# A second run of Strassen quads in a decoder trunk's output projections

## The chip, the cores and the metric

The kernel runs on one core of one Trainium2 chip. The metric is the device time of one execution in microseconds, from the median of several runs; less is better. Engines are named as in the profile: PE (TensorE), PEld (its weight loads), DVE (VectorE), ACT (ScalarE), POOL (GpSimd) and SP (the queue that issues most loads). Each engine takes its own list of instructions in order.

## The reference

Two decoder layers over 256 tokens of width 2048, all in float32. Each layer is attention, an output projection `attn @ w_o`, a residual with layer norm, a gated feed-forward with a width-3 convolution, its down projection, and another residual with layer norm:

```python
for layer in range(DEPTH):                                  # DEPTH = 2
    attn = moba_attention(h, ..., moba_w_o) or swa_attention(..., swa_w_o)
    ...                                                     # both end in  o.reshape(B, S, ATT_WIDTH) @ w_o
    h = layer_norm(ALPHA * h + attn, ln_g[layer, 0], ln_b[layer, 0])
    ffn = conv_ffn(h, w_up, conv_w, conv_b, w_down)
    h = layer_norm(ALPHA * h + ffn, ln_g[layer, 1], ln_b[layer, 1])
```

The change is in the two output projections: 256 x 2048 times 2048 x 2048, one after each attention.

## The kernel before, in words

**Three products for one.** Each float32 factor is held as a high part (`wh`, rounded to the fast format) and a low part (`wl`, what is left). A product is three matmuls that add into one PSUM bank: high by high, high by low, low by high (L502 to L504). The weights stream from HBM in *halves* of 128 x 1024 (two blocks of 128 x 512, 512 KB). SP loads a half into one of six `raw` buffers, ACT copies it to `wh` (L173), DVE subtracts to get `wl` (L182). This pair is called the *split* of a half. `wh` and `wl` have four buffers, so as a rule the split of half i + 4 waits until PE is done with half i. Before the end of a projection the list `reach` lets the splits run further ahead: halves then go into parts of `xT`, `st` and `up` that stand empty.

**Tokens and chunks.** The 256 tokens are two tiles (t = 0, 1) of 128, and the 2048 output columns are four chunks (n = 0 to 3) of 512. A *plain* half is multiplied with both token tiles: 2 blocks x 2 tiles x 3 = 12 matmuls.

**Quads.** Where two contraction blocks, two chunks and the two token tiles meet, the kernel may use a Strassen scheme with 7 products in place of 8. Two quads are worked off as seven *mixed* halves (`SEVEN`), each with 2 x 3 = 6 matmuls. Three of the seven come from the weights themselves and four (T1 to T4) from sums of weight blocks. `presums` makes these sums in earlier stages on DVE (L449, four of 128 x 512 for a quad), and sends them through HBM (`gb` in, `ws` out on POOL, `ws` back in as `raw`). The token side needs sums too: `sums` makes them per pair of quads from the attention's output (`st`) and puts them in `xT` (`whole` L539, `combine` L550, `split` L555 and L556).

**Folding.** In a run of quads, PSUM holds P1, P5, P6 and P7 for the chunk pair (tiles named `at`, four banks) beside the direct results (tiles `acc`, four banks). When the pair's quads are done, `fold` adds the four into the residual `res` in three steps (`first`, `second`, `third`), each run behind one more half. `into` does one such addition, and a BN_STATS (L623) when the last part of a token tile and chunk has come. A bank is free for the next user when its last reader is done. `evac` adds a direct result to `res`.

**Order.** All orders are written out by hand: `at(n, f)` puts `f` n halves later, and `take` first issues the splits up to the half now wanted plus three (or `reach`), then what `at` has due. What was put in first is in the engine's list first.

An output projection has 38 halves before (numbered from 0 here): 5 plain, 7 mixed, 3 plain and 7 mixed for chunks 0 and 1 (four quads), then 16 plain halves for chunks 2 and 3. The last eight are the *window*: all eight with t = 0 first, and then all with t = 1, so that tile 0's norm (`late`: `evac`, `moments`, `norm`, L630 to L642) and the transposes for the next stage (`turn`, L675) can start while PE does t = 1. In the window the splits run ahead to the first six halves of the next stage.

Attention's last steps hang over into the first halves of the projection; the last head's `values` (L824, L825) and `outputs` (ACT L829, DVE L830) are of these, and they hold one of the four `at` banks.

Of the kernel before, what the change touches and what calls it, by code (L numbers as in the profile page):

```python
# [47 lines left out]
NQ = 12  # L48
PLAINS = ((5, 2, 2, 2, 2, 0, 6), (0, 1, 1, 1, 1, 0, 15))
NQ_O = 4  # L50
PLAINS_O = (5, 3, 0)
IN_PARTS = (True, True)
NV = 2 * 8 + 4 * 8
SEVEN = (("B11", "B21"), ("T1", "T3"), ("T2", "T4"), ("B22", "B22"), ("B11", "B21"), ("T1", "T3"), ("T2", "T4"))
# [19 lines left out]
    return plan  # L74


PLAN_O = _mixed(0, PLAINS_O, _plain(range(NH - 2 * NQ_O), (0, 1)), NH // 2 - NQ_O) + _plain(range(NH), (2, 3))
PLAN_V = _mixed(1, PLAINS_O, _plain(range(KB - 2 * NQ_O), (2, 3)), KB // 2 - NQ_O)
PLAN_DOWN = [h for c in range(2) for h in _mixed(c, PLAINS[c], _plain(range(2 * NQ, FT), (2 * c, 2 * c + 1)), 0)]
QUADS = {}  # L80
for _l in range(2):
    QUADS[2 * _l] = [(2 * _l, 0, NH // 2 - NQ_O + p) for p in range(NQ_O)]
    QUADS[2 * _l + 1] = [(2 * _l + 1, c, p) for c in range(2) for p in range(NQ)]
QUADS[4] = [(4, 1, KB // 2 - NQ_O + p) for p in range(NQ_O)]
ORDER = [q for li in (4, 0, 1, 2, 3) for q in QUADS[li]]
AHEAD_OF = {0: QUADS[4] + QUADS[0] + QUADS[1][:2], 1: QUADS[1][2:] + QUADS[2], 2: [], 3: QUADS[3]}


def _summed(half):
# [22 lines left out]
def trunk(ctx: ExitStack, tc: tile.TileContext, wst, wsum, xT_in, x_in, relb, onehot, umask, sinks, conv_in, ln_g, ln_b, out):  # L112
# [353 lines left out]
    def mixed(src, plan, p0, ns, quad_blocks, place, into):  # L466

        banks, used, owed = {}, {}, {}

        def token(x, t):  # L470
            return x[:, t * P:(t + 1) * P], x[:, T + t * P:T + (t + 1) * P]

        def keys(e):
            b, k, n = e
            if b == "plain":
                return [(n, t) for t in range(2)]
            n0, n1 = 2 * n, 2 * n + 1
            return [{"B11": ("P1", n), "B21": (n0, 0), "T1": ("P5", n), "T3": ("P7", n), "T2": ("P6", n), "T4": (n0, 1),
                     "B22": (n1, 0)}[b]]

        def target(e):
            b, k, n = e
            if b == "plain":
                return [(key, *token(src(k), t)) for t, key in enumerate(keys(e))]
            k1, k2, far = src(2 * k), src(2 * k + 1), place((k - p0) // 2)
            far = [tuple(far[:, h, k % 2, j, :] for h in range(2)) for j in range(ns)]
            s1, s3, s4, s2 = (far[0], token(k1, 1), *far[1:]) if ns == 3 else far
            return [(*keys(e), *{"B11": token(k1, 0), "B21": token(k2, 0), "T1": s1, "T3": s3, "T2": s2,
                                 "T4": token(k2, 1), "B22": s4}[b])]

        for half in plan:
            for e in half:
                for key in keys(e):
                    owed[key] = owed.get(key, 0) + 1

        def product(key, sh, sl, wh, wl):
            if key not in banks:
                banks[key] = psum.tile([P, 512], F32, name="at" if key[0] in SUMS else "acc")
                used[key] = 0
            acc, first, last = banks[key], used[key] == 0, used[key] == owed[key] - 1  # L500
            used[key] += 1
            nc.tensor.matmul(acc, sh, wh, start=first, stop=False)  # L502
            nc.tensor.matmul(acc, sh, wl, start=False, stop=False)  # L503
            nc.tensor.matmul(acc, sl, wh, start=False, stop=last)  # L504

        def done(*keys):
            return all(used.get(key) == owed[key] for key in keys)

        def fold(c):
            n0, n1 = 2 * c, 2 * c + 1  # L510
            p1, p5, p6, p7 = (banks.pop((b, c)) for b in SUMS)
            w = tmpp.tile([P, HW], F32, name="tmp")
            u, v = w[:, 0:512], w[:, 512:HW]

            def first():
                nc.scalar.activation(u, p1, AF.Copy)
                into(0, n0, u)
                nc.vector.tensor_tensor(out=u, in0=p6, in1=u, op=ALU.add)
                nc.vector.tensor_tensor(out=v, in0=p5, in1=u, op=ALU.add)

            def second():
                into(0, n1, v)
                nc.vector.tensor_tensor(out=u, in0=p7, in1=u, op=ALU.add)

            def third():
                into(1, n0, u)
                into(1, n1, u)
                into(1, n1, p5)

            for i, f in enumerate((first, second, third)):  # L530
                at(1 + i, f)

        def sums(i):
            x = quad_blocks(i)
            g = []

            def whole():
                g.append(tmpp.tile([P, HW], F32, name="tmp"))
                nc.vector.tensor_tensor(out=g[0].rearrange("p (a b) -> p a b", a=4), in0=x[:, :, 0:T].bitcast(F32),  # L539
                                        in1=x[:, :, T:2 * T].bitcast(F32), op=ALU.add)  # L540

            def combine():
                a11, a21, a12, a22 = (g[0].rearrange("p (q s c) -> p s q c", q=2, s=4)[:, j] for j in range(4))
                if ns == 3:
                    ops = (a22, a22, a21, ALU.subtract), (a21, a22, a11, ALU.add), (a12, a12, a22, ALU.subtract)
                else:
                    ops = ((a21, a11, a21, ALU.subtract), (a22, a22, a21, ALU.subtract), (a11, a22, a11, ALU.add),
                           (a12, a12, a22, ALU.subtract))
                for o, a, b, op in ops:
                    nc.vector.tensor_tensor(out=o, in0=a, in1=b, op=op)  # L550

            def split():
                s = g[0].rearrange("p (q s c) -> p q s c", q=2, s=4)[:, :, 4 - ns:4, :]
                hi, lo = (place(i)[:, h] for h in range(2))
                nc.scalar.activation(hi, s, AF.Copy)  # L555
                nc.vector.tensor_tensor(out=lo, in0=s, in1=hi.bitcast(F32), op=ALU.subtract)  # L556

            return whole, combine, split

        return SimpleNamespace(banks=banks, target=target, product=product, done=done, fold=fold, sums=sums)  # L560

    def project_out(src, plan, li, homes, preload, turnover=None, quad_blocks=None):
# [13 lines left out]
        def settle():  # L576


            ring, places, following = homes()
            aside.update({w0 - len(ring) + j: x for j, x in enumerate(ring) if x})  # L580
            aside.update({w0 + j: x for j, x in enumerate(places)})
            aside.update({n0 + 4 + j: x for j, x in enumerate(following)})
            first = w0 - len(ring) - AHEAD
            for i in range(first, w0 + 3):
                reach[i] = i + min(AHEAD + (i - first) * 3 // 5, len(ring) - 1)
            for i, s in enumerate((4, 6, 7, 9, 11, 12, 13), w0 - 4):
                reach[i] = min(max(reach[i], w0 + s), n0 + 5)

        stats = stat.tile([P, 2, NCH, 6], F32, name="stats", bufs=1, padded_shape=[P, 2, NCH, 10])
        gb = gbp.tile([P, 2, D], F32, name="gb")  # L590
# [107 lines left out]

        def late(t, i):
            last = i == WINDOW - 1  # L700
            if t == 0 and last:
                evac(NCH - 1, 0)
                sd = moments(0)
                nc.vector.reciprocal(rs[0], sd)
                for c in COLS[0]:
                    norm(0, c)
            if t == 1 and after:
                if 3 <= i < 7:
                    c = COLS[0][i - 3]
                    low(0, c, turn(0, c))  # L710
                if 5 <= i < 7:
                    high_upto(n0 + i + 1)
            if t == 1 and last:
                evac(NCH - 1, 1)
                if after:
                    sd = moments(1)
                    nc.vector.reciprocal(rs[1], sd)
                else:
                    last_norm()
            if t == 1 and not after and 2 <= i < NCH + 1:  # L720
                scaled_ahead(i - 2)

        if quads:
            groups = PLAINS[0] if ns == 3 else PLAINS_O
            for i in range(len(groups) - 1):
                m = 4 if i and not groups[i] else sum(groups[:i]) + 7 * i - (ns == 3) if i else ns == 3
                for j, f in enumerate(sums(i)):
                    at(m + j, f)
        evacuated, folded = set(), set()
# [112 lines left out]
    def layer_attention(l, rest, stage, turnover):  # L842
# [65 lines left out]
        def v_pair():  # L908
# [17 lines left out]

            parted = mixed(src, PLAN_V, k0 // 2, 4, lambda i: xT[:, k0 + 4 * i:k0 + 4 * i + 4, :], place, into)
            mv = Moving(src, 0)
            for i in range(len(PLAINS_O) - 1):
                for j, f in enumerate(parted.sums(i)):  # L930
                    at(sum(PLAINS_O[:i]) + 7 * i + j, f)
            evacuated = set()
            for half in PLAN_V:
                blocks = [mv.block() for _ in range(2)]
# [53 lines left out]
    class FeedForward:  # L988
# [31 lines left out]
        def run(self, rest):  # L1020
# [62 lines left out]

            ws_opening(accs, between, opened)
            ahead = AHEAD_OF[2 * l + 1]
            presums(ahead, [4 + 152 * i // (len(ahead) - 1) for i in range(len(ahead))])
            for u in range(OPENING, 2 * FT):
                acc = acc_tile()
                ws_unit(acc)
# [137 lines left out]
```

## Time and profile before

| | before |
|---|---|
| median of three runs | 2043.67 us (2043.19 to 2043.96) |
| the profiled execution | 2042.94 us, of which its span is 2041.2 us |
| PE, PEld busy | 2034.1 us, 1759.5 us |
| DVE, ACT, POOL busy | 1722.3 us, 1162.5 us, 79.7 us |
| matmuls | 10962 |
| DMA | 578.20 MB, mean 283 GB/s |
| granted TensorE clock | 1.000 |

The profile is one execution by the hardware profiler; its own time is 0.73 us under the median of the runs. Busy times are per engine and overlap. Matmuls are pipelined: a 128 x 512 matmul has a duration of 0.39 us in the rows, but the next one starts 0.23 us later, so distances between starts are what counts. In the timeline, "x2" is two instructions in one row, and brackets show the idle time before the first and what ended it. The first output projection lies at 292 to 381 us, the second at 1240 to 1331 us.

### The profile page before, as it was taken

The numbers are of one execution on the slowest core, as the hardware profiler recorded it, in microseconds if no ns is written. First come the engines' busy times: TensorE is split into PE (matmuls) and PEld (weight loads), VectorE is DVE, ScalarE is ACT, GpSimd is POOL, SyncE is SP. The second block draws the span as 40 slices with busy tenths as digits, with TensorE's granted clock in tenths as the row PEclk, the third lists the DMA queues.
The fourth block names the chain that finished last, engine by engine and source line by source line (L and its number), as shares of the span: only waits on it lengthen the run. The fifth ranks groups of instructions, "written<-read, shape, count | busy, mean of one in ns | idle before, by whom it ended". The sixth has DMA issues, their size and how long they took to land.

```text
span 2041.2 us, 30207 instructions
## 1 busy us (share of the span) xinstructions
PE 2034.1 (100%) x10962; PEld 1759.5 (86%) x10962; DVE 1722.3 (84%) x2520; ACT 1162.5 (57%) x1762; POOL 79.7 (4%) x146
## 2 busy tenths in 40 slices
PE   9999999999999999999999999999999999999999
PEld 8888888988888888888888888898888888888886
DVE  6778889888888888899896788978888888889887
ACT  5556556455555555566663566545555555566673
POOL 0100000000000000000000000000000000000000
PEclk9999999999999999999999999999999999999999
DMA  8988888578888899889995546748888888879894
GB/s 302 314 299 313 299 301 292 176 250 319 313 319 298 316 320 315 296 289 328 330 358 200 168 151 207 280 137 295 297 309 303 311 299 300 302 263 330 313 358 164
DMA packets 161893, 578.20 MB, mean 283 GB/s; under 512 B 19360, under 2 KB 21728, under 8 KB 160464
## 3 DMA queue, kind: packets, MB, share of 16 engines
q1 hardware_dynamic: 138080, 500.08, 71.1%
q0 software_dynamic: 21312, 73.84, 9.1%
q10 hardware_dynamic: 2352, 2.36, 0.4%
q8 instruction: 86, 1.41, 0.3%
q14 instruction: 63, 0.52, 0.1%
HBM read 511.12 MB, written 69.26 MB: 284 GB/s over the span
## 4 chain that ended last, share of the span: by engine, by line
PE 98%; DVE 1%; DMA 0%; ACT 0%; issue 0%; DVEq 0%
PE acc L335 39%; PE acc L337 20%; PE acc L504 8%; PE acc L502 8%; PE acc L503 8%; PE at L503 3%; PE at L504 3%; PE at L502 3%; PE acc L362 2%; PE acc L399 1%; PE acc L400 1%; PE acc L398 1%; PE acc L374 1%; PE at L675 1%; PE at L807 1%; DVE wl L182 0%
## 5 line engine op out<-in xcount | busy, mean ns | idle before, releaser
L182 DVE TENSOR_TENSOR wl<-raw,wh 128x1024 fp32r<-128x1024 f32 (+1 forms) x760 | 905.5, 1219 | 163.0 <-ACT wh L173 140.2
L173 ACT ACTIVATE wh<-raw 128x1024 fp32r<-128x1024 f32 (+1 forms) x760 | 777.1, 1053 | 195.4 <-PE acc L504 113.2
L335 PE MATMUL acc<-xT,wh 128*128 128x512 f32 x3456 | 830.6, 392 | 0.0
L335 PEld LDWEIGHTS acc<-xT,wh 128*128 128x128 f32 x3456 | 640.8, 188 | 127.4
L337 PEld LDWEIGHTS acc<-xT,wl 128*128 128x128 f32 x3456 | 443.7, 190 | 12.5
L337 PE MATMUL acc<-xT,wl 128*128 128x256 f32 x3456 | 449.4, 283 | 0.0
L1041 ACT ACTIVATE h<-acc 128x256 f32<-128x256 f32 x172 | 66.0, 384 | 409.2 <-PE acc L337 203.1
L1049 DVE SCALAR_TENSOR_TENSOR c<-h,cw,c 128x255 f32<-128x255 f32 x344 | 165.4, 481 | 9.1 <-ACT c L1045 2.8
L449 DVE TENSOR_TENSOR gb<-gb 128x512 f32<-128x512 f32 x240 | 164.2, 684 | 0.0
L1042 DVE TENSOR_TENSOR h<-acc,h 128x256 f32<-128x256 f32 x172 | 72.5, 421 | 49.0 <-ACT h L1041 48.7
L453 POOL DMA_DIRECT2D ws<-gb x120 | 64.0, 533 | 1263.8 <-DVE gb L449 1126.2
L502 PE MATMUL acc<-wh,up 128*128 128x512 f32 x275 | 107.0, 389 | 0.0
L503 PE MATMUL acc<-wl,up 128*128 128x512 f32 x275 | 107.0, 389 | 0.0
L504 PE MATMUL acc<-wh,up 128*128 128x512 f32 x275 | 107.0, 389 | 0.0
L1045 ACT ACTIVATE c<-h,cw 128x256 f32<-128x256 f32 x172 | 101.8, 592 | 0.0
L502 PE MATMUL acc<-wh,st 128*128 128x512 f32 x178 | 70.4, 395 | 0.0
L504 PE MATMUL acc<-wh,st 128*128 128x512 f32 x178 | 69.4, 390 | 0.0
L503 PE MATMUL acc<-wl,st 128*128 128x512 f32 x178 | 69.3, 389 | 0.0
L503 PEld LDWEIGHTS acc<-wl,up 128*128 128x128 f32 x275 | 51.6, 188 | 10.7
L504 PEld LDWEIGHTS acc<-wh,up 128*128 128x128 f32 x275 | 51.6, 188 | 10.7
L502 PEld LDWEIGHTS acc<-wh,up 128*128 128x128 f32 x275 | 51.6, 188 | 10.6
L954 ACT ACTIVATE qT<-acc 128x256 f32<-128x256 f32 x32 | 12.3, 384 | 58.4 <-PE acc L337 41.6
(231 smaller groups left out, 2245.1 us busy)
## 6 DMA issues: line engine op xcount, KB each, us to landing
raw<-in_wst_dram SPq DMA_DIRECT2D x692, 512.0 KB, 5.2
gb<-in_wsum_dram SPq DMA_DIRECT2D x120, 512.0 KB, 6.9
ws<-gb POOLq DMA_DIRECT2D x120, 512.0 KB, 6.2
raw<-ws SPq DMA_DIRECT2D x120, 512.0 KB, 5.8
bias<-band POOLq DMA_DIRECT2D x8, 512.0 KB, 8.3
band<-ud POOLq DMA_DIRECT2D x4, 512.0 KB, 11.7
band<-ud ACTq DMA_DIRECT2D x4, 512.0 KB
res<-in_x_dram SPq DMA_DIRECT2D x2, 1024.0 KB, 7.8
```

The costliest lines, as they stand in the source:

```text
L173: nc.scalar.activation(wh[:, c], raws[s][:, c], AF.Copy)
L182: nc.vector.tensor_tensor(out=wl[:, c], in0=raws[s][:, c], in1=wh[:, c].bitcast(F32), op=ALU.subtract)
L335: nc.tensor.matmul(acc, w, xT[:, k, :], start=(k == 0), stop=(k == ends[0]))
L337: nc.tensor.matmul(acc[:, 0:T], w, xT[:, k, 0:T], start=False, stop=(k == ends[1]))
L449: nc.vector.tensor_tensor(out=w[:, o:o + 512], in0=a, in1=b, op=op)
L502: nc.tensor.matmul(acc, sh, wh, start=first, stop=False)
L503: nc.tensor.matmul(acc, sh, wl, start=False, stop=False)
L504: nc.tensor.matmul(acc, sl, wh, start=False, stop=last)
L1041: nc.scalar.activation(h, acc[:, T:2 * T], AF.Copy)
L1042: nc.vector.tensor_tensor(out=h, in0=acc[:, 0:T], in1=h, op=ALU.add)
L1045: nc.scalar.activation(c, h, AF.Identity, bias=w[:, 3:4], scale=w[:, 2:3])
L1049: nc.vector.scalar_tensor_tensor(c[:, d:T], h[:, 0:T - d], w[:, 2 - d:3 - d], c[:, d:T], op0=ALU.mult, op1=ALU.add)
```

## The change

Both output projections get two more quads, in the second chunk pair (chunks 2 and 3), on contraction blocks 12 to 15. The plan has 41 halves now: 4 plain, 7 mixed, 2 plain, 7 mixed and 2 plain for the first pair; 1 plain, 7 mixed and 11 plain for the second. The token sums in `xT` are those of the first pair's second run, so they are kept longer, and one entry of `reach` is lowered by one for that. Two halves of chunk 2 fall into the window now, so `late` looks for finished results there. `fold` reads P5 in its second step rather than its third. The value projection keeps its old groups (`PLAINS_V`). The presums of the four new quads are spread anew: the first attention makes ten as before, the first feed-forward 27 for 26, the second attention 3 for none, the second feed-forward 24 as before.

```diff
 NQ_O = 4
-PLAINS_O = (5, 3, 0)
+PLAINS_O = (4, 2, 2)
+PLAINS_V = (5, 3, 0)
...
-PLAN_O = _mixed(0, PLAINS_O, _plain(range(NH - 2 * NQ_O), (0, 1)), NH // 2 - NQ_O) + _plain(range(NH), (2, 3))
-PLAN_V = _mixed(1, PLAINS_O, _plain(range(KB - 2 * NQ_O), (2, 3)), KB // 2 - NQ_O)
+PLAN_O = _mixed(0, PLAINS_O, _plain(range(NH - 2 * NQ_O), (0, 1)), NH // 2 - NQ_O) + _mixed(
+    1, (1, 11), _plain(range(NH - NQ_O), (2, 3)), NH // 2 - 2)
+PLAN_V = _mixed(1, PLAINS_V, _plain(range(KB - 2 * NQ_O), (2, 3)), KB // 2 - NQ_O)
...
-    QUADS[2 * _l] = [(2 * _l, 0, NH // 2 - NQ_O + p) for p in range(NQ_O)]
+    QUADS[2 * _l] = [(2 * _l, c, NH // 2 - NQ_O + p) for c in range(2) for p in range(2 * c, NQ_O)]
...
-AHEAD_OF = {0: QUADS[4] + QUADS[0] + QUADS[1][:2], 1: QUADS[1][2:] + QUADS[2], 2: [], 3: QUADS[3]}
+AHEAD_OF = {0: QUADS[4] + QUADS[0], 1: QUADS[1] + QUADS[2][:3], 2: QUADS[2][3:], 3: QUADS[3]}
...
             def second():
                 into(0, n1, v)
+                into(1, n1, p5)
                 nc.vector.tensor_tensor(out=u, in0=p7, in1=u, op=ALU.add)
 
             def third():
                 into(1, n0, u)
                 into(1, n1, u)
-                into(1, n1, p5)
...
+            if ns == 4:
+                reach[w0 - 4] = min(reach[w0 - 4], w0 + 3)
...
         def late(t, i):
             last = i == WINDOW - 1
+            for n in range(NCH - 1):
+                if (n, t) not in evacuated and done((n, t)):
+                    evacuated.add((n, t))
+                    evac(n, t)
...
-                m = 4 if i and not groups[i] else sum(groups[:i]) + 7 * i - (ns == 3) if i else ns == 3
+                m = 4 if i and not groups[i] else sum(groups[:i]) + 7 * i - (groups[i] == 2) if i else ns == 3
...
-            presums(ahead, [4 + 152 * i // (len(ahead) - 1) for i in range(len(ahead))])
+            presums(ahead, [4 + 156 * i // (len(ahead) - 1) for i in range(len(ahead))])
```

Three places show how instructions move. First PE, at the start of the first output projection: the last head's `values` (`at<-PT,vt`) against the first mixed half (`at<-wh,st` is P1, the first `at<-wh,xT` is P5). Before:

```order
L504 MATMUL acc<-wh,st 128x512
L824 MATMUL at<-PT,vt 128x256
L825 MATMUL at<-PT,vt 128x128
L502 MATMUL at<-wh,st 128x512
L503 MATMUL at<-wl,st 128x512
L504 MATMUL at<-wh,st 128x512
L502 MATMUL acc<-wh,st 128x512
L503 MATMUL acc<-wl,st 128x512
L504 MATMUL acc<-wh,st 128x512
L502 MATMUL at<-wh,xT 128x512
```

And after (all lines from the functions here on stand two to eight further down):

```order
L815 MATMUL at<-ident,L 128x128 x3
L504 MATMUL at<-wh,st 128x512
L505 MATMUL at<-wl,st 128x512
L506 MATMUL at<-wh,st 128x512
L504 MATMUL acc<-wh,st 128x512
L505 MATMUL acc<-wl,st 128x512
L506 MATMUL acc<-wh,st 128x512
L832 MATMUL at<-PT,vt 128x256
L833 MATMUL at<-PT,vt 128x128
L504 MATMUL at<-wh,xT 128x512
```

`values` stood ahead of the whole mixed run, and stands behind its first half now, so that the last head's bank is read out while the run is under way.

Second DVE, where the first pair is folded (`tmp<-at,tmp` are the sums of `fold`, `res<-res,tmp` and `res<-res,at` its additions, `res<-res,acc` an `evac`, and rows out of `raw` are splits). Before, among the plain halves of chunk 2:

```order
L617 TENSOR_TENSOR res<-res,tmp 128x512
L623 BN_STATS stats<-res 128x6
L518 TENSOR_TENSOR tmp<-at,tmp 128x512
L519 TENSOR_TENSOR tmp<-at,tmp 128x512
L182 TENSOR_TENSOR wl<-raw,wh 128x1024
L617 TENSOR_TENSOR res<-res,tmp 128x512
L623 BN_STATS stats<-res 128x6
L523 TENSOR_TENSOR tmp<-at,tmp 128x512
L182 TENSOR_TENSOR xT<-raw,xT 128x1024 x2
```

And after, the rows from the split of half 24 to the second-last step of the fold:

```order
L184 TENSOR_TENSOR xT<-raw,xT 128x1024
L623 SCALAR_TENSOR_TENSOR res<-res,tmp 128x512
L623 SCALAR_TENSOR_TENSOR res<-res,at 128x512
L526 TENSOR_TENSOR tmp<-at,tmp 128x512
L621 TENSOR_TENSOR res<-res,acc 128x512
L627 BN_STATS stats<-res 128x6
L621 TENSOR_TENSOR res<-res,acc 128x512
L184 TENSOR_TENSOR xT<-raw,xT 128x1024
L184 TENSOR_TENSOR up<-raw,up 128x1024
L621 TENSOR_TENSOR res<-res,tmp 128x512
L627 BN_STATS stats<-res 128x6
L621 TENSOR_TENSOR res<-res,tmp 128x512
```

The fold and the evacuations of the first pair stand between the splits of halves 24 to 28 now, which are the new mixed run's (23 to 29).

Third DVE again, the rows ahead of tile 0's norm in the window (BN_AGGR begins `moments`). Before:

```order
L182 TENSOR_TENSOR up<-raw,up 128x1024 x3
L182 TENSOR_TENSOR wl<-raw,wh 128x1024 x2
L619 SCALAR_TENSOR_TENSOR res<-res,acc 128x512
L623 BN_STATS stats<-res 128x6
L619 SCALAR_TENSOR_TENSOR res<-res,acc 128x512
L623 BN_STATS stats<-res 128x6
L182 TENSOR_TENSOR wl<-raw,wh 128x1024 x2
L182 TENSOR_TENSOR up<-raw,up 128x1024 x2
L619 SCALAR_TENSOR_TENSOR res<-res,acc 128x512
L623 BN_STATS stats<-res 128x6
L630 BN_AGGR ag<-stats 128x2
```

And after:

```order
L526 TENSOR_TENSOR tmp<-at,tmp 128x512
L184 TENSOR_TENSOR wl<-raw,wh 128x1024 x2
L623 SCALAR_TENSOR_TENSOR res<-res,tmp 128x512
L621 TENSOR_TENSOR res<-res,tmp 128x512
L184 TENSOR_TENSOR wl<-raw,wh 128x1024 x2
L184 TENSOR_TENSOR up<-raw,up 128x1024
L621 TENSOR_TENSOR res<-res,acc 128x512
L627 BN_STATS stats<-res 128x6
L184 TENSOR_TENSOR up<-raw,up 128x1024
L621 TENSOR_TENSOR res<-res,acc 128x512
L627 BN_STATS stats<-res 128x6
L634 BN_AGGR ag<-stats 128x2
```

The new pair's fold stands between the next stage's splits (the last `wl` and `up` rows), all of it still ahead of tile 0's last evacuation; chunk 2's second tile is evacuated behind the norm now.

More of the change, by code (lines that the diff above doesn't have):

```diff
@@ L928, in v_pair @@
             mv = Moving(src, 0)
-            for i in range(len(PLAINS_O) - 1):
+            for i in range(len(PLAINS_V) - 1):
                 for j, f in enumerate(parted.sums(i)):
-                    at(sum(PLAINS_O[:i]) + 7 * i + j, f)
+                    at(sum(PLAINS_V[:i]) + 7 * i + j, f)
             evacuated = set()
```

## Prediction

> **What bounds the kernel now.** I read the page's busy times and its chain first, then the busy times by stretch, the waits, and last the timeline of the two output projections.
>
> ```profile
> span 2041.2 us, 30207 instructions
> PE 2034.1 (100%) x10962; PEld 1759.5 (86%) x10962; DVE 1722.3 (84%) x2520; ACT 1162.5 (57%) x1762; POOL 79.7 (4%) x146
> PE 98%; DVE 1%; DMA 0%; ACT 0%; issue 0%; DVEq 0%
> ...
> 290.00:382.00 92.00, 92.00 (x429) 76.55 (x428) 85.18 (x111) 55.77 (x69) 2.13 (x4) 1.00 0.79 281
> 382.00:860.00 478.00, 478.00 (x2804) 424.40 (x2804) 407.15 (x633) 260.80 (x426) 27.18 (x51) 1.00 0.85 295
> 1105.00:1234.00 129.00, 129.00 (x787) 114.97 (x787) 93.75 (x219) 71.84 (x179) 3.70 (x6) 1.00 0.57 187
> ...
> 329.02:369.75 40.73, 40.73 (x182) 33.73 (x181) 40.45 (x46) 26.39 (x27) 0.00 (x0) 1.00 0.83 298
> 1278.29:1319.22 40.93, 40.93 (x183) 33.89 (x182) 40.55 (x45) 26.38 (x27) 0.00 (x0) 1.00 0.84 297
> ...
> PEld at L675 <- DVE res L642: 0.7, 2, 0.4
> ...
> PE at L503 <- DVE wl L182: 0.6, 2, 0.3
> ```
>
> The rows by stretch give the length, then PE, PEld, DVE, ACT, POOL, the granted clock and DMA. Over the whole, PE is the bound. But in each output projection there is a stretch of 41 us, from the second mixed run to tile 0's last evacuation, in which DVE is busy for 40.5 us too. The last two rows are of the waits (total, times, longest): in both projections the weight load of the first `turn` on PE (L675) already waits for DVE's norm (L642), and no wait for a `wl` inside the run is over 0.3 us. So the two engines are level there, and what DVE gets on top comes out at PE.
>
> **What PE saves.** 6 matmuls in each projection (2 quads x 3). Their distance:
>
> ```profile
> 317.77 0.39 PE L502 MATMUL acc<-wh,st 128*128 128x512 f32 x1
> ...
> 329.78 0.39 PE L504 MATMUL acc<-wh,st 128*128 128x512 f32 x1
> ```
>
> These are 54 matmuls without a gap: 12.01 / 53 = 0.2266 us each. A mixed half is 1.36 us, a plain one 2.72, the saving 1.36 a projection and **2.72 us** in all.
>
> **What DVE gets.** In a projection: three more splits (41 halves for 38), three sums in `fold`, five additions into `res`; two of the old operations, the evacuation of chunk 2's second tile and its BN_STATS, move behind the norm. So ahead of tile 0's last `evac` come 3 splits and 6 operations of 128 x 512. From start to start:
>
> ```profile
> 332.42 0.68 DVE L619 SCALAR_TENSOR_TENSOR res<-res,acc 128x512 f32<-128x512 f32 x1
> 333.02 1.22 DVE L182 TENSOR_TENSOR xT<-raw,xT 128x1024 fp32r<-128x1024 f32 x1
> 335.89 2.35 DVE L182 TENSOR_TENSOR up<-raw,up 128x1024 fp32r<-128x1024 f32 x2
> 338.16 1.22 DVE L182 TENSOR_TENSOR wl<-raw,wh 128x1024 fp32r<-128x1024 f32 x1
> 342.16 0.68 DVE L617 TENSOR_TENSOR res<-res,tmp 128x512 f32<-128x512 f32 x1
> 342.88 0.69 DVE L623 BATCH_NORM_STATS2 stats<-res 128x6 f32<-128x512 f32 x1
> ...
> 369.75 0.68 DVE L619 SCALAR_TENSOR_TENSOR res<-res,acc 128x512 f32<-128x512 f32 x1
> ...
> 373.53 0.63 PE L675 MATMUL at<-ident,res 128*128 128x128 f32 x4
> ...
> 1319.22 0.68 DVE L619 SCALAR_TENSOR_TENSOR res<-res,acc 128x512 f32<-128x512 f32 x1
> ...
> 1322.97 0.66 PE L675 MATMUL at<-ident,res 128*128 128x128 f32 x4
> ```
>
> A split takes 1.135 us (two in 2.27), an operation 0.60, or 0.72 where the next one reads its result: 0.64 on average. As a check, 329.02 to 369.75 holds 25 splits and 20 operations: 28.4 + 12.4 = 40.8 us against 40.73. The added work is 3 x 1.135 + 6 x 0.64 = 7.2 us, against 1.36 us less of PE.
>
> [...]
>
> **Where it comes out, first projection.** I walk along the order with these distances. *The front:* the mixed run begins at half 4, which in these rows of before (PE, ACT, DVE) is still a plain one, from 304.71 to 307.56.
>
> ```profile
> 304.71 0.48 PE L502 MATMUL acc<-wh,st 128*128 128x512 f32 x1
> 307.56 0.59 PE L824 MATMUL at<-PT,vt 128*128 128x256 f32 x2
> 308.13 0.48 PE L502 MATMUL at<-wh,st 128*128 128x512 f32 x1
> 310.97 0.39 PE L502 MATMUL at<-wh,xT 128*128 128x512 f32 x1
> ...
> 307.81 1.06 ACT L173 ACTIVATE wh<-raw 128x1024 fp32r<-128x1024 f32 x1 [1.96 <-issue]
> 308.78 0.37 ACT L829 ACTIVATE st<-at 128x256 fp32r<-128x256 f32 x1
> ...
> 308.90 1.23 DVE L182 TENSOR_TENSOR wl<-raw,wh 128x1024 fp32r<-128x1024 f32 x1 [2.11 <-ACT wh L173]
> 310.05 0.42 DVE L830 TENSOR_TENSOR st<-at,st 128x256 fp32r<-128x256 f32 x1
> ```
>
> P6 (310.97 here) takes the last head's bank, which DVE frees at 310.47; now two mixed halves lie between, not three halves with a plain one. Half 4 ends at 304.71 + 1.36 + 0.13 = 306.20; split 8 and `outputs` follow it as they follow 307.56 here, so the bank is free at 310.47 - 1.36 = 309.11, while P6's half would start at 308.25 (306.20, 0.57 for `values`, one mixed half, and 0.12 that the first matmul behind `values` takes longer). **+0.9 us** (0 to 1.3). *The sums:* `whole` to the end of `split` takes 5.2 us without the wait in it:
>
> ```profile
> 320.21 1.22 DVE L539 TENSOR_TENSOR tmp<-st 128x1024 f32<-128x1024 f32 x1
> 321.79 1.23 DVE L182 TENSOR_TENSOR wl<-raw,wh 128x1024 fp32r<-128x1024 f32 x1 [0.36 <-ACT wh L173]
> 325.74 1.23 DVE L556 TENSOR_TENSOR xT<-tmp,xT 128x1024 fp32r<-128x1024 f32 x1
> ...
> 327.54 1.06 ACT L173 ACTIVATE wh<-raw 128x1024 fp32r<-128x1024 f32 x1 [0.30 <-PE acc L504]
> ```
>
> It had three plain halves, and has a mixed one and two plain ones. The last row shows the ring: ACT starts 0.25 us after PE has left half i - 4, and `wl` is there 2.56 us after it (0.25 + 1.06 + 0.03 + 1.22). By that `whole` starts at 317.1 and the low part ends at 323.5, where PE wants it for half 14 at 323.2. **+0.4 us** (0 to 0.6). Half 19 then starts at X = 309.15 + 5 x 1.36 + 2 x 2.72 + 6 x 1.36 + 0.4 = 330.0.
>
> *The ramp:* split 21 starts at X, and from there DVE never waits. Up to the start of split 27 stand splits 21 to 26 and 16 operations (four `evac`, three sums and five additions of the fold, four BN_STATS): 6.8 + 10.2 = 17.0; `wl` 27 is there at X + 18.2. PE wants it after half 19, three plain and four mixed halves and one matmul: X + 15.2. **+3.0 us.** P5, which is read one step sooner, is free at X + 9.7, and half 24 wants it at X + 10.9; that is no wait.
>
> *The window:* up to tile 0's last `evac` stand 26 splits and 26 operations: 29.5 + 16.6 = 46.1, at 376.0, where before it was 369.75. `turn` follows 3.78 us later, at 379.8 for 373.53. **+6.3 us** in all; of it the front 0.9, the sums 0.4, the ramp 3.0, the rest (3.3) at the first `turn`, less 1.36 saved. From there to the stage's end nothing new is late: `evac` (2, t = 1) pushes the `low` rows 1.3 us back, and the last of them comes about 0.7 us ahead of its reader.
>
> The second projection has the same order: `evac` 1319.22 goes to 1325.3, `turn` 1322.97 to 1329.1, **+6.1**.
>
> **What costs nothing.** The presums: 16 operations of 0.68 us more, 8 loads on SP, 8 stores on POOL. Three quads (8.2 us) go to the second attention, where DVE has 35 of 129 us idle, one to the first feed-forward, with 71 of 478 us idle. SP's raw loads stand behind those 8, but the second attention moves 187 GB/s, far under the 298 of the window, so they stay ahead. Behind POOL's stores in the second attention stand two loads of bias, for heads that come later. Their bounds are 0 and +2. For the three added raw loads of a projection, 298 GB/s was met with DVE as reader; DVE reads no faster now, so 0, at most +1.
>
> **Sum:** 6.3 + 6.1 = +12.4 on the profiled execution's 2042.94 us is 2055.3; that one lies 0.73 under the median, so against the median 2043.67 it is **2056.0 us**. With both fronts and sums at 0 it is +9.8, with all upper ends +16.
>
> **Rivals.** (1) *PE's count decides:* 2043.67 - 2.72 = 2041.0, not slower. It would need DVE's added work to pass behind the norm. For it speaks the page, with DVE at 84%. Against it the order: all six next-stage splits (6.8 us) stand ahead of the last `evac`. It holds only if 7.2 us of idle time turned up in stretches with 0.3. 12%. (2) *Part of it is taken up:* the front and the sums (1.3) cost nothing, and DVE makes up 2 us in the first mixed runs, where it idles now (2.11 us in the row at 308.90). Then it is +3 a projection, 2050. Against it: those gaps are waits for the ring, not for DVE. 14%. (3) *The clock drops after the waits:* four waits of about 3 us, where the trace has one of 0.3 us at most inside the run and 1.000 throughout. If the matmuls ran at twice the distance for as long as a wait lasted, each would lose 1.5 us: +6 on top, 2062. 6%. [...]
>
> **How the numbers follow.** The forecast has 64%, the rivals 12, 14 and 6, and 4% are left for a small change for reasons that I don't see. Range: 2049 to 2061, which holds the forecast with its bounds, most of (2) and part of (3). 0.2% is 4.1 us, about what a measurement here can tell. Slower by more: forecast, (2) and (3), 84%. Rival (1), at -0.13%, lies within it: same 13%, faster 3%.
>
> **What would show it.** Right: PE idle by 4 to 8 us in each projection, waits of PE or PEld on `wl` L184 near half 27 and on `res` L646 at the first `turn`, and DVE without idle time between them. The front shows as a wait of a matmul of P6 on DVE `st`. Wrong: a first `turn` without a wait of over 1 us and a shorter projection, or a wait in the attentions, which would mean that the presums weigh.

## The result, and the profile after

The changed kernel takes 2065.82 us (median of five runs, 2064.38 to 2067.37), the kernel before 2043.67 in the same session: a ratio of 1.0108, 95% interval 1.0097 to 1.0119. It is 22 us slower; 12 were forecast, and 2061 was the upper end of the range. The profiled execution took 2064.38 us, 21.4 us more than that of before.

From the page of the changed kernel come the span, the busy times with their counts, and the chain's shares:

```profile
span 2062.6 us, 30278 instructions
...
PE 2038.5 (99%) x10950; PEld 1758.6 (85%) x10950; DVE 1749.0 (85%) x2558; ACT 1170.0 (57%) x1770; POOL 84.1 (4%) x154
...
PE 91%; DVE 6%; issue 1%; DMA 1%; ACT 1%; DVEq 0%
```

PE has the 12 matmuls less, and still 4.4 us more of busy time; DVE has 6% of the chain for 1%. The place is found by cutting both traces at the same matmuls. These are the two output projections and the two down projections (columns: stretch and length, then PE, PEld, DVE, ACT, POOL, granted clock, DMA share, GB/s), of before:

```profile
291.84:380.87 89.03, 89.03 (x410) 73.81 (x409) 82.38 (x105) 54.33 (x68) 1.60 (x3) 1.00 0.80 288
862.92:1083.24 220.32, 220.03 (x979) 181.58 (x977) 198.14 (x206) 143.61 (x145) 0.00 (x0) 1.00 0.88 316
1240.34:1330.33 89.99, 89.99 (x414) 74.39 (x412) 83.00 (x108) 54.37 (x69) 0.54 (x1) 1.00 0.72 251
1812.37:2030.83 218.46, 218.17 (x962) 180.00 (x961) 190.93 (x199) 133.47 (x133) 0.00 (x0) 1.00 0.82 294
```

and of the changed kernel:

```profile
292.29:391.45 99.16, 90.34 (x404) 73.44 (x403) 91.19 (x116) 57.96 (x72) 1.61 (x3) 0.98 0.78 272
873.49:1095.12 221.63, 220.66 (x979) 181.44 (x978) 199.84 (x209) 143.60 (x145) 1.07 (x2) 1.00 0.88 318
1252.27:1349.94 97.67, 91.56 (x407) 74.00 (x406) 91.17 (x119) 58.03 (x73) 0.54 (x1) 0.98 0.72 249
1831.99:2051.70 219.71, 218.75 (x962) 179.88 (x961) 192.44 (x202) 133.35 (x133) 1.07 (x2) 1.00 0.83 295
```

The output projections are 10.1 and 7.7 us longer, the down projections 1.3 and 1.25. The feed-forwards between them are the same to 0.01 us. About 1 us is left: the first projection starts 0.45 us later, as it did by 0.2 to 0.8 in every later run of this study, one without new quads among them, and 0.5 lies behind the last stage.

The waits of PE (total, times, longest):

```profile
PE at L679 <- DVE res L646: 8.4, 2, 5.5
PE at L505 <- DVE up L184: 3.8, 2, 1.9
PE at L504 <- DVE st L838: 1.4, 2, 0.8
PE at L505 <- DVE xT L184: 1.3, 2, 0.7
```

All four rows belong to places that were forecast: the front (0.9 forecast, 0.75 and 0.64 found), the ramp near half 27 (3.0 forecast; 1.89 and 0.67 found, in both projections) and the first `turn`. At the sums 0.4 was forecast, and 0.02 is there. Not forecast were two waits in the down projections, of 0.33 and 0.35 us in the first. The timeline of PE shows them in brackets:

```profile
309.60 0.50 PE L504 MATMUL at<-wh,xT 128*128 128x512 f32 x1 [0.75 <-DVE st L838]
348.69 0.50 PE L505 MATMUL at<-up,st 128*128 128x512 f32 x1 [1.89 <-DVE up L184]
382.81 1.12 PE L679 MATMUL at<-ident,res 128*128 128x128 f32 x4 [5.49 <-DVE res L646]
383.57 0.78 PE L504 MATMUL acc<-xT,st 128*128 128x512 f32 x1
1342.57 0.66 PE L679 MATMUL at<-ident,res 128*128 128x128 f32 x4 [2.88 <-DVE res L646]
```

Counted from each projection's start, the first `turn` went from 81.69 to 90.52 us and from 82.63 to 90.30, by 8.8 and 7.7 us, where 6.3 and 6.1 were forecast. Two things went differently. First, DVE is not without idle time behind the fold. The rows of DVE, ACT and SP, first projection:

```profile
349.80 1.47 SPq L156 DMA_DIRECT2D raw<-in_wst_dram  x2
354.23 1.22 DVE L184 TENSOR_TENSOR xT<-raw,xT 128x1024 fp32r<-128x1024 f32 x1
355.45 1.06 ACT L175 ACTIVATE xT<-raw 128x1024 fp32r<-128x1024 f32 x1 [2.22 <-DVE xT L184]
356.54 2.52 DVE L184 TENSOR_TENSOR xT<-raw,xT 128x1024 fp32r<-128x1024 f32 x2 [1.10 <-ACT xT L175]
359.84 1.23 DVE L184 TENSOR_TENSOR up<-raw,up 128x1024 fp32r<-128x1024 f32 x1 [0.78 <-ACT up L175]
379.05 0.68 DVE L621 TENSOR_TENSOR res<-res,acc 128x512 f32<-128x512 f32 x1
```

DVE waits for ACT's copy, and ACT by its bracket for DVE; but that split had nothing to do with this copy (in the last experiment below ACT makes the same copy before that split begins). The copy also waits for its raw load, which SP could issue only at 349.80, when a split behind the fold had freed a buffer. The DMA part of the page for 340 to 375 us has the median landing:

```profile
raw<-in_wst_dram SPq DMA_DIRECT2D x19, 512.0 KB, 5.4
```

349.80 + 5.4 is 355.2. Second, PE itself was slow for a while; by stretch:

```profile
340.00:345.00 5.00, 4.33 (x19) 3.30 (x18) 4.97 (x8) 2.42 (x3) 0.00 (x0) 1.00 0.37 109
355.00:360.00 5.00, 5.00 (x24) 4.14 (x23) 3.05 (x4) 3.18 (x3) 0.00 (x0) 1.00 0.98 373
382.80:385.45 2.65, 2.64 (x9) 2.26 (x10) 2.58 (x4) 0.60 (x1) 0.00 (x0) 0.50 0.02 8
1310.60:1313.90 3.30, 3.30 (x10) 2.52 (x9) 3.30 (x4) 1.61 (x2) 0.00 (x0) 0.50 0.95 278
```

The first two rows are the loads: 109 GB/s while DVE folds, 373 at 0.98 of the engines when it splits again. The last two show a granted clock of 0.50, behind the first `turn` in one projection and behind the ramp in the other; the matmuls there start 0.427 us apart, not 0.227.

### The profile page after: what moved, and what is told of

It is laid out like the page before. It is cut to its first block, busy times and chain, and to the rows that moved or that the text cites. A ratio compares the mean times of both kernels' runs of the same rounds, so it can differ in the third digit from the quotient of the medians.

```text
span 2062.6 us, 30278 instructions
## 1 busy us (share of the span) xinstructions
PE 2038.5 (99%) x10950; PEld 1758.6 (85%) x10950; DVE 1749.0 (85%) x2558; ACT 1170.0 (57%) x1770; POOL 84.1 (4%) x154
## 4 chain that ended last, share of the span: by engine, by line
PE 91%; DVE 6%; issue 1%; DMA 1%; ACT 1%; DVEq 0%
PE acc L337 38%; PE acc L339 20%; PE acc L504 6%; PE acc L506 6%; PE acc L505 6%; PE at L505 2%; PE at L506 2%; PE at L504 2%; DVE wl L184 2%; PE acc L364 1%; PE acc L401 1%; PE acc L400 1%; PE acc L402 1%; DMA raw<-in_wst_dram 1%; PE acc L376 1%
## 5 line engine op out<-in xcount | busy, mean ns | idle before, releaser
L451 DVE TENSOR_TENSOR gb<-gb 128x512 f32<-128x512 f32 x256 | 175.2, 684 | 0.0
L455 POOL DMA_DIRECT2D ws<-gb x128 | 68.5, 535 | 1393.2 <-DVE gb L451 1267.6
```

The source lines that it names most:

```text
L451: nc.vector.tensor_tensor(out=w[:, o:o + 512], in0=a, in1=b, op=op)
L455: nc.gpsimd.dma_start(wsums[q][:, js], w[:, js])
```

## The experiments

Every time is a median with its range; each ratio is to the kernel before, run beside it.

**The presums of the feed-forwards spread as before.**

```diff
-            presums(ahead, [4 + 156 * i // (len(ahead) - 1) ...
+            presums(ahead, [4 + 152 * i // (len(ahead) - 1) ...
```

> The changed kernel with one number set back: the presums of the feed-forward stages are spread over 152 places, not 156. In the changed kernel each down projection is 1.3 us longer (221.62 us for 220.32, and 219.71 for 218.46); two new waits of PE of 0.33 and 0.35 us stand there, and the last quad's four presums run on DVE inside the down projection, 2 to 13 us after its start. Theory: those four operations are the whole cause, so both down projections fall back to 220.3 and 218.5 us and the time to 2065.8 - 2.5 = 2063.3. Rival: the new order of the fold's steps, which the down projections share, is the cause; then nothing moves, 2065.8.

2084.79 us (2083.55 to 2086.10). With 27 quads in 152 places some neighbours stand five apart, and their steps interleave in the one buffer `gb`: sums are made of the wrong blocks, DVE stands still for the loads, and the first feed-forward is 21 us longer. The total says nothing, then, but the down projections stand by themselves:

```profile
895.53:1115.87 220.34, 220.05 (x979) 181.54 (x978) 198.11 (x206) 143.71 (x145) 0.00 (x0) 1.00 0.88 315
1854.20:2072.79 218.59, 218.31 (x962) 179.90 (x961) 190.56 (x199) 133.46 (x133) 0.00 (x0) 1.00 0.83 294
```

They (both rows by stretch) are back at the lengths of before, to 0.02 and 0.13 us, with the fold's new order still in them. So the presums' place costs 2.5 us, and the fold's order nothing there. In the changed kernel the last presum stands among the down projection's first sums and splits, and PE waits soon after (timeline of DVE and PE):

```profile
885.66 0.69 DVE L451 TENSOR_TENSOR gb<-gb 128x512 f32<-128x512 f32 x1
893.28 0.50 PE L505 MATMUL at<-wl,st 128*128 128x512 f32 x1 [0.33 <-DVE wl L184]
895.29 0.49 PE L505 MATMUL at<-wl,xT 128*128 128x512 f32 x1 [0.35 <-DVE wl L184]
```

0.68 us of waits cost 1.30 us of stage. From the start of the last matmul ahead of a wait to the one behind it pass 0.39 us more than the wait, where 0.23 is usual, and the next one starts 0.34 us behind that: some 0.27 us on top of each wait.

**Four of the next stage's splits behind tile 0's norm.**

```diff
-                reach[i] = min(max(reach[i], w0 + s), n0 + 5)
+                reach[i] = min(max(reach[i], w0 + s), n0 + (1 if ns == 4 else 5))
...
+                if ns == 4 and i < 2:
+                    high_upto(n0 + 3 + 2 * i)
...
-                    if i > OPENING:
-                        split_upto(n0 + i + 1)
+                    split_upto(n0 + 3 + 2 * (i - OPENING))
```

> The changed kernel with four of the six splits of the next stage (halves n0+2 to n0+5) taken out from ahead of tile 0's last evacuation; ACT still copies them in the second half of the window, DVE makes their low parts in the feed-forward's opening, where they are read late. Theory (DVE's queue): 4 x 1.135 = 4.5 us less ahead of the norm, so the wait at the first turn goes from 5.5 and 2.9 us to about 1.0 and 0, and with the first the stretch at half the clock behind it (1.5 us): 2065.8 - 9.2 = 2056.6. Rival (refill of the raw buffers is what holds the norm back): the last evacuation comes 1 us sooner at most, 2063 to 2065. Rival (given back later): the waits at turn go, but the feed-forward's opening has new ones on the low parts of 3 us or more, 2060 or above.

2056.23 us (2054.90 to 2057.24), 1.0059 (1.0047 to 1.0072): 9.6 us under the changed kernel by the medians, where 9.2 was expected, though the two profiled executions are only 7.3 apart. The wait at `turn` is gone in both projections, where 1.0 was expected in the first. The timeline of PE has no bracket there:

```profile
378.60 0.60 PE L679 MATMUL at<-ident,res 128*128 128x128 f32 x4
```

The first feed-forward by stretch:

```profile
385.92:868.75 482.83, 482.30 (x2833) 428.28 (x2832) 417.12 (x645) 263.92 (x430) 27.72 (x52) 1.00 0.86 301
```

Nothing of the wait is left because PE now came there later itself: in this run the clock was halved behind the ramp's wait in both projections (0.50 from 349.60 to 352.90 us in the first, and from 1305.30 to 1308.60 in the second), and with DVE out of the way that lengthened the projection. So the total agrees with the expectation in part by luck. The opening of each feed-forward gave back 0.8 us (482.83 for 482.04). DVE's list ahead of the norm is what set the `turn`.

**Matmuls that add nothing, in the waits.**

```diff
+            for _ in range(n):
+                nc.tensor.matmul(banks[key][0:64, :], zero, src(0), start=False, stop=False)
...
+                    if t and i == 3 and ns == 4:
+                        fill((NCH - 1, 1), (10, 20)[li == 0])
...
+            if ns == 4 and i == 26:
+                fill((NCH - 1, 0), 6)
```

> The changed kernel with matmuls of a zero weight (128 x 64, adding nothing) put on PE where it waits anyway: 6 behind half 26 (ahead of the wait on half 27's low part), and 20 and 10 ahead of the first turn of the first and second projection, where PE waits for 5.5 and 2.9 us. DVE's list is the same but for two operations at the start. Theory (part of the cost is the clock: behind these waits 7 and 8 matmuls run at 0.427 us for 0.227, granted clock 0.50): the waits shrink by what the fill takes, no stretch at 0.5 is left, and the time falls by 7 x 0.2 + 8 x 0.2 = 3.0 us to 2062.8. Rival: the slow matmuls have another cause, and the time stays at 2065.8.

2063.99 us (2063.39 to 2065.41), 1.0098 (1.0085 to 1.0112). The gain of 1.8 us lies within what the two intervals leave open; the profile is clearer; the two projections by stretch, with the granted clock in the third column from the end:

```profile
292.21:390.43 98.22, 95.07 (x431) 75.85 (x430) 90.60 (x116) 57.97 (x72) 1.60 (x3) 1.00 0.78 275
1251.22:1349.93 98.71, 93.69 (x424) 75.01 (x422) 91.14 (x119) 57.88 (x73) 0.54 (x1) 1.00 0.70 246
```

No stretch at half the clock is left. The first `turn` of the first projection:

```profile
383.06 0.66 PE L683 MATMUL at<-ident,res 128*128 128x128 f32 x4 [1.19 <-DVE res L650]
```

From there to the stage's end it takes 7.4 us again, as in before, for 8.64 in the changed kernel: the 1.3 us are the clock's. The second projection gained nothing. There the slow stretch lay ahead of the wait at `turn`, so it had only taken the place of a wait. It even took longer (98.71 us for 97.67), because DVE idled 1.1 us more behind the fold, at copies that wait for raw loads, and the `turn` came as much later. Half of the expected 3.0 us was therefore wrong: a slow PE costs where PE is late, not where DVE is.

**The first pair's grouping alone, on the kernel before.**

```diff
-PLAINS_O = (5, 3, 0)
+PLAINS_O = (4, 2, 2)
```

> The kernel before with the first chunk pair's groups alone changed from 5, 3, 0 to 4, 2, 2 plain halves, and no new quads, presums or other edit. Theory: this carries the changed kernel's two early waits (P6 on the last head's bank, 0.75 and 0.64 us, and one of 0.02 us on the sums), each with about 0.28 us for emptying and refilling PE's pipeline: 2043.7 + 1.4 + 4 x 0.28 = 2046.2. Rival: these waits come from elsewhere (presums, DVE's load), and the regrouping is free: 2043.7.

2045.90 us (2045.71 to 2046.18), 1.0009 (1.0000 to 1.0018). The median is 2.2 us over before, though the interval just reaches no change; the profile settles it, with the waits of 0.75 and 0.64 us at P6 and of 0.02 at the sums, and projections of 90.36 and 91.13 us for 89.03 and 89.99. The front is the grouping's price, without any new quad.

**The fold's old order of steps.**

```diff
             def second():
                 into(0, n1, v)
-                into(1, n1, p5)
...
                 into(1, n1, u)
+                into(1, n1, p5)
```

> The changed kernel with the fold's old order of steps: P5 is read last, in the third step. In the changed kernel P5 is read at 339.40 to 340.0 us, and the half that writes its bank next starts at 340.0. Theory: by the order of DVE's list P5 would be read at about 347, so PE waits some 7 us there; the waits behind it (2.6 us) vanish, and the later splits, which need buffers that PE frees, come about 4 us later, so does the first turn: 2065.8 + 2 x 4 = 2074. Rival: DVE's list sets the turn and PE's waits inside the run are only moved about: 2065.8, with the old order's down projections unchanged.

2065.17 us (2063.57 to 2067.56), 1.0107 (1.0093 to 1.0121): the rival, and not the theory. In the timeline of PE, first projection:

```profile
347.05 0.77 PE L504 MATMUL at<-xT 128*128 128x512 f32 x1 [4.18 <-DVE res L621]
...
382.92 0.66 PE L679 MATMUL at<-ident,res 128*128 128x128 f32 x4 [1.47 <-DVE res L646]
```

and the stretch behind the wait:

```profile
347.00:352.90 5.90, 5.85 (x14) 4.62 (x15) 5.90 (x6) 2.16 (x3) 0.00 (x0) 0.50 0.64 206
```

PE waits 4.2 us for the bank (ahead of half 25; the forecast had half 24 want it), loses another 2.6 at half the clock for 5.9 us, and then comes to a `turn` that stands where it stood (90.65 us from the start for 90.52, and 90.71 for 90.30 in the second projection). What PE loses inside the run is taken off the wait at its end. So the earlier release of P5 gains nothing here: it moves a wait.

**The second run one plain half later** (groups 2, 10 for 1, 11).

```diff
-    1, (1, 11), _plain(range(NH - NQ_O), (2, 3)), NH // 2 - 2)
+    1, (2, 10), _plain(range(NH - NQ_O), (2, 3)), NH // 2 - 2)
```

> The changed kernel with the second chunk pair's groups 2, 10 for 1, 11: its mixed run begins one plain half later, so its fold's third step (two additions into tile 1's res) falls behind tile 0's norm. Theory (the turn is set by DVE's list, the wait inside the run by how early PE asks): the wait near half 27 falls from 2.6 us to about 1.0, and the norm comes 2 x 0.64 = 1.3 us sooner in each projection, so the turn too: 2065.8 - 2.6 = 2063.2. Rival (only the place in PE's list matters): the full 1.6 us of the wait are gained in each projection, 2062.6 with the same norm; or nothing moves, since the raw loads hold DVE: 2065.8.

2070.69 us (2068.92 to 2071.79). It doesn't answer the question: the run ends one half later, the guard in `reach` wasn't moved with it, and the copy of half w0 + 4 overwrites the token sums (in `xT`) of the last mixed half, which computes with the wrong ones, 7.4 us late. Ahead of that the wait near half 27 fell from 2.56 to 1.51 us, where 1.0 was expected.

**Behind the norm, and the presums mended.** The second run's kernel with 152 places, 26 quads in the first feed-forward and four in the second attention.

```diff
-AHEAD_OF = {..., 1: QUADS[1] + QUADS[2][:3], 2: QUADS[2][3:], ...
+AHEAD_OF = {..., 1: QUADS[1] + QUADS[2][:2], 2: QUADS[2][2:], ...
```

> The run with four splits behind the norm (2056.2), and the presums mended: the feed-forwards spread theirs over 152 places again, for which the first takes 26 quads and the second attention four. Theory: the down projections fall back to 220.3 and 218.5 us as in the run with 152 places, the second attention has room for one quad more, and nothing else moves: 2056.2 - 2.5 = 2053.7. Rival: the fourth quad in the second attention makes PE wait there or in the projection behind it, 2054.5 or more.

2053.86 us (2053.09 to 2055.00), 1.0050 (1.0038 to 1.0063): 2.4 us for 2.5. The down projections measure 220.31 and 218.43 us, and the second attention has no wait.

**Low parts on POOL.** The second run's kernel, with the splits of halves 22, 24 and 26 finished on POOL.

```diff
-        nc.vector.tensor_tensor(out=wl[:, c], in0=raws[s][:, c], ...
+        eng = nc.gpsimd if s in on_pool else nc.vector
+        eng.tensor_tensor(out=wl[:, c], in0=raws[s][:, c], ...
...
+            on_pool.update(w0 + WINDOW - len(plan) + x for x in (22, 24, 26))
```

> The run with four splits behind the norm (2056.2), and the low parts of the projections' halves 22, 24 and 26 made on POOL, not DVE: 3 x 1.135 = 3.4 us off DVE's list where the fold stands among the splits. Theory: the waits of 0.7 and 1.9 us inside the second run go, with them the stretch at half the clock (1.6 us) and the restarts (0.5 us), and the turn comes about 4 us sooner in each projection: 2056.2 - 8 = 2048. Rival: a subtraction of 128 x 1024 on POOL takes so long, or slows DVE's operations beside it so much, that the halves it makes are late themselves: 2056 or more.

2053.54 us (2051.38 to 2056.39), 1.0053 (1.0039 to 1.0066): a third of the expected gain, all of it in the second projection (91.03 us for 94.55; the first 94.05 for 93.82). In the first, one addition of the first pair's fold met a subtraction on POOL, as the timeline shows:

```profile
334.67 2.72 POOL L185 TENSOR_TENSOR xT<-raw,xT 128x1024 fp32r<-128x1024 f32 x1 [0.62 <-ACT xT L175]
335.06 2.89 DVE L624 TENSOR_TENSOR res<-res,tmp 128x512 f32<-128x512 f32 x1
```

It took 2.89 us for 0.68, and PE waited 2.15 us behind it. DVE's operations that read PSUM were not slowed: two sums out of `at`, at 338.59 and 339.30, took 0.67 and 0.69 us beside the next subtraction on POOL (337.36 to 340.23), for 0.68 and 0.69 on average in before. The addition ended 0.56 us after the subtraction on POOL that ran beside it, and one in the next run did too (2.90 us, until 337.12, with POOL at work until 336.56). In three rows of the two runs a split on DVE that started beside a subtraction on POOL took 2.38, 2.56 and 2.69 us for 1.22, and ended 1.08 or 1.09 us after that. Where the DVE operation was first, the subtraction on POOL took 2.72 to 2.87 us, for the 2.40 and 2.41 of the first ones of this run in the two projections.

**All together.** The seventh run's kernel with the opening's splits placed a little later, and halves 8, 13, 21, 22, 24 and 26 on POOL.

> All that helped so far in one kernel with the new quads: four splits behind the norm (their low parts a little later in the opening than in the first such run, where PE waited 0.53 us), the presums as in the run that measured 2053.9, and the low parts of the projections' halves 8, 13, 21, 22, 24 and 26 on POOL. Half 8's split stands just ahead of the last head's output on DVE, half 13's among the sums. Theory: from 2053.9 go the front's waits (0.75 and 0.64, and 0.28 for a restart each: 2.0), the sums' restart (0.6), the waits and slow stretches inside the run (about 3.3 a projection), the opening's (2 x 0.8): 2053.9 - 2.0 - 0.6 - 6.6 - 1.6 = 2043.1, as fast as before. Rival: POOL's subtractions stall DVE (in the last run one of DVE's additions took 2.89 us for 0.68 while POOL was at work), and the gain inside the run is half as large: 2047.

2049.56 us (2049.07 to 2050.19), 1.0029 (1.0017 to 1.0040). It is the fastest kernel with the new quads, and still 5.8 us over before, over the rival even. The two projections by stretch:

```profile
292.63:384.67 92.04, 89.21 (x404) 72.30 (x403) 83.51 (x106) 57.63 (x72) 18.66 (x9) 1.00 0.77 270
1244.22:1336.37 92.15, 89.98 (x407) 72.80 (x406) 84.26 (x109) 57.69 (x73) 17.58 (x7) 1.00 0.68 240
```

The front's waits are gone, and no stretch is slow. In either projection 0.8 us twice inside the run and 0.5 us at the sums are left, and in the first 0.65 us at `turn`. There, in the first, DVE's addition took 2.90 us beside POOL, and its split at the sums 2.69. The projections are 3.0 and 2.2 us longer than in before.

**Half of the raw loads left out behind the fold.**

```diff
-            raws[u] = wpool.tile([P, HW], F32, name="raw")
-            for j, c in enumerate(pieces(u)):
+            raws[u] = raws[u - 1] if u in shared else wpool.tile(...)
+            for j, c in enumerate(() if u in shared else pieces(u)):
...
+            shared.update(w0 + WINDOW - len(plan) + x for x in (30, 32, 34, 36, 38, 40))
```

> The changed kernel without the raw loads of halves 30, 32, 34, 36, 38 and 40 of each projection: they are split from the buffer of the half before, so their weights are the wrong ones; all copies, splits and matmuls stay. Theory (the term that was sized 0 to 1): behind the fold DVE idles 2.0 and 1.0 us and its splits are 0.1 us further apart, because a raw buffer comes free only after the fold and its load takes 5.5 us; without half of those loads DVE's list runs through, and the first turn comes 90.5 - 2.5 = 88.0 and 90.3 - 1.5 = 88.8 us after the projection's start. The time is 2065.8 - 4 = 2061.8. Rival: DVE waits there for buffers that PE frees, or for ACT; then the turn stays at 90.4 us and the time at 2065.8.

2058.61 us (2058.49 to 2060.75), 1.0076 (1.0064 to 1.0089). From its timeline, ACT's copies of three halves, their splits on DVE behind the fold, DVE's last evacuation ahead of the norm, and PE's first `turn` in either projection:

```profile
346.90 3.08 ACT L175 ACTIVATE xT<-raw 128x1024 fp32r<-128x1024 f32 x3 [2.51 <-DMA raw<-in_wst_dram]
...
354.04 3.49 DVE L184 TENSOR_TENSOR xT<-raw,xT 128x1024 fp32r<-128x1024 f32 x3
...
376.30 0.68 DVE L623 TENSOR_TENSOR res<-res,acc 128x512 f32<-128x512 f32 x1
380.06 0.66 PE L681 MATMUL at<-ident,res 128*128 128x128 f32 x4 [1.33 <-DVE res L648]
1336.86 0.66 PE L681 MATMUL at<-ident,res 128*128 128x128 f32 x4 [2.89 <-DVE res L648]
```

From split 21 to tile 0's last evacuation DVE idles 0.28 us in either projection, all in gaps below 0.06 us, where the changed kernel has 2.31 and 1.30. ACT has made its three copies by 349.98, before the first of their splits begins at 354.04. The `turn` comes 88.0 and 88.7 us after the start, for 90.5 and 90.3. That is 6.3 and 6.1 us later than in before, the forecast's own figures. So the refill of the raw buffers is the whole rest of that term. The run takes away six loads a projection, so it shows what loading behind the fold costs, and not what the three added loads cost by themselves. The total fell by more than expected; in the profile 1.3 us of it is the slow stretch, which here lies inside the run, ahead of a wait.

## Why the forecast was right, and where it failed

The direction and the mechanism stood: DVE's list sets the first `turn`, and what it gets on top comes out at PE. The start of half 19 was forecast 38.2 us behind the projection's start, and came there, in part by luck: the waits of 0.77 us ahead of it were 0.5 short of the forecast, and the 0.27 us that each of two waits costs on top, which the forecast didn't have, made up for it. The walk along DVE's list put tile 0's last evacuation 84.2 us behind the start; without half of the loads it stood at 84.25. (For before, the prediction counts 20 operations where the rows hold 19; at the 0.65 us that these take its 12.4 us are the same.) PE's saving was real, and rivals (1) and (2) fell.

Three steps failed:

- **The added raw loads, "0, at most +1".** Waiting for raw loads behind the fold cost 2.5 us in the first projection and 1.6 in the second. The step took the mean rate (298 GB/s, with DVE as reader) and concluded that DVE would read no faster. But DVE reads in bursts. While it folds, the six raw buffers stay full and little is loaded (109 GB/s); then the splits come 1.135 us apart, while a half of 512 KB takes 1.4 us at the 373 GB/s that were reached there (an estimate from that rate), and DVE waits. "From there DVE never waits" was wrong by 2.0 and 1.0 us of idle time.
- **The presums, "what costs nothing".** Their number was counted, and their cover in the attention and the feed-forward was real. But in the feed-forwards 152 became 156 places, and the last quad moved into the down projection, where DVE has no slack: 2.55 us in all, over the stated bound of +2.
- **The clock, a rival at 6%.** It came about, with another price. Two stretches of 3.41 us at 0.50 were found. The twofold distance was an assumption of the forecast, which no row of before shows; in these stretches the matmuls stand 0.427 us apart for 0.227. The estimate of 1.5 us for each wait was near what one such stretch takes from PE (7 x 0.2 = 1.4 us by its matmuls, half of 3.41 = 1.7 by its length), but only the one behind the first `turn` lengthened the program, by 1.3 us.

4.1 (the raw loads, 2.5 and 1.6), 2.55 and 1.3, and the 1.0 at the two ends, are 8.95 us; the profiled execution, at 2064.38, is 9.1 over the 2055.3 that the forecast made of it. The median lies another 1.4 us above. The profiled execution has a mean granted clock of 0.998, the four others of 0.997 and times of 2065.55 to 2067.37, so they have more of the slow stretches; where these lie is not shown. It goes the same way in the second run: 2054.90 and 2055.68 us at 1.000, 2057.12 and 2057.24 at 0.998.

The sizes within the walk were fair: front 0.75 and 0.64 for 0.9, ramp 2.56 for 3.0. P5's release, held for no wait, is none; but the fifth run shows that it would not have mattered either way.

## What to carry to other kernels

Where one engine's list sets the end of a stage, a wait of another engine inside that stage is only moved, so judge each edit by what it adds to that list ahead of the deciding operation. A block of other work in a stream of loads can cost twice, as the fold did here: its own time, and then the refill, since loads wait when buffers aren't freed (109 GB/s while DVE folds here, 373 behind it); check the rate before and behind the block, not its mean. Every number that shifts a schedule, however small, has to be followed to the last instruction that it moves.

## What the runs showed of the hardware

- The granted clock fell to 0.50 behind some waits of PE, and not behind others as long. In the changed kernel it fell behind the ramp's wait of 1.89 us in the second projection, and not behind the one of 1.89 us in the first; it fell behind the first `turn`'s 5.49 us, and not behind the second's 2.88. Of eight projections with a ramp wait of about 1.9 us (the changed kernel, the second, the seventh and the last run) six have a stretch at 0.50 behind it, and two have none. In the last run the clock stayed at 1.00 behind the 2.89 us at the second `turn`, and in the fifth it fell behind the 4.2 us in both projections. With matmuls of zero weight in the waits it was 1.00 throughout both projections, the second with 3.2 us of wait left at `turn`. The length of one wait does not decide it.
- In the changed kernel's trace the two stretches at 0.50 inside the program last 3.413 us each, from 382.18 us, 0.63 us ahead of the wait's end, and from 1310.60. The stretches at 1.00 last 375.466, 925.012 and 747.519 us, which are 110, 271 and 219 times 3.4133. In the 3.42 us ahead of the second drop PE was busy for 1.53 us, with the whole ramp wait among them, and in the 3.41 ahead of the first not at all. A stretch as long in the first projection holds 1.24 us of the ramp's wait; there PE was busy for 2.18 us, and the clock stayed. The rows are that stretch, the one ahead of the second drop, and the one behind it:

```profile
344.62:348.04 3.42, 2.18 (x10) 1.47 (x8) 3.35 (x6) 0.92 (x1) 0.00 (x0) 1.00 0.88 255
1307.18:1310.60 3.42, 1.53 (x7) 0.97 (x6) 3.39 (x5) 1.57 (x2) 0.00 (x0) 1.00 0.55 165
1310.60:1314.01 3.41, 3.41 (x10) 2.63 (x9) 3.41 (x4) 1.61 (x2) 0.00 (x0) 0.50 0.95 277
```

- A wait of PE cost about 0.27 us more than its length in the changed kernel, at waits of 0.33, 0.35, 0.67 and 1.89 us: from the last matmul ahead of it to the first one behind it pass 0.39 us more than the wait, and from that to the next 0.33 or 0.34, for the usual 0.23.
- A subtraction of 128 x 1024 took POOL 2.40 and 2.41 us at its shortest (DVE: 1.22). Two additions and three splits on DVE with two inputs in SBUF, started beside one, ended 0.56 and 1.08 or 1.09 us after it, 1.2 to 2.2 us late. Where the DVE operation was first, the subtraction on POOL took up to 2.87 us.
